# Hybrid attention layer: attention outputs in DRAM per head, with the two contributions as neighbouring rows

## Chip, cores and metric

One Trainium2 chip, one NeuronCore. The metric is the device time of one execution of the whole program in microseconds (us). The time before is the median of three executions, 1822.48 us (1818.33 to 1823.29).

## What is computed

One layer of a decoder trunk over 1024 tokens of width 2048, all in float32. The reference, cut to its outline:

```python
u = rmsnorm(h, norm_pre[l])
proj = jnp.einsum('bsd,de->bse', u, w_in[l])                  # 2048 -> 6656
q_sb, k_sb, v_sb, z_sb, q_sw, k_sw, v_sw, z_sw = jnp.split(proj, SPLIT_POINTS, axis=-1)
o_sb = stick_breaking_attention(q_sb, k_sb, v_sb)             # 16 heads of 64
o_sw = sliding_window_gqa(q_sw, k_sw, v_sw, sinks[l], rel_bias)  # 16 heads, 4 kv heads, window 128
o_sb = rmsnorm(o_sb, gn_sb[l]) * jax.nn.silu(z_sb)
o_sw = rmsnorm(o_sw, gn_sw[l]) * jax.nn.silu(z_sw)
y = jnp.einsum('bse,ed->bsd', jnp.concatenate([o_sb, o_sw], axis=-1), w_out[l])
h = h + rmsnorm(y, norm_post[l])
```

## The kernel before, in words

**Number format.** A matmul of two float32 operands is made of three faster matmuls: each operand is split into a rounded high part and a low rest (`hi`, `lo`; `xh`, `xl`), and hi*hi, hi*lo and lo*hi are added up in PSUM. In attention the high and the low part of a 64-wide head lie side by side on the 128 partitions, so that one matmul takes both.

**Phase 1, projections.** The list `work` (L727) holds 49 blocks of 128 output columns; `proj` (L450) computes each with 96 matmuls of 128x512. Weights come in four pieces of 256 KB per block (`split_w`, L128: a load on SP's queue, a cast on ACT, a subtraction on VectorE). What follows a block depends on its kind: q and k are scaled, split and spilled to DRAM (`split_spill`, L371); v is transposed and kept; z is the gate (`evac_z`, L412).

**Attention in the gaps.** After every three matmuls of a projection `step` (L252) calls `advance` (L148), which places pieces of attention units between the projection matmuls by an estimate of TensorE's time and by written-out lags. A unit has three stages: `s1` makes logits and weights, `s2` transposes the weights on TensorE and splits them, `s3` multiplies them with v into PSUM tile `o`. The order on TensorE is the program's order; on the other engines and on SP's queue, a scheduler orders the instructions at build time, by program order, priorities and its own estimate of when each is ready, and every engine and queue then works strictly in that order. In time, the sliding-window units (`sw`, 64 of them) come first, up to about 490 us, and the stick-breaking units (`sb`, 160) follow, to about 1450 us.

**Attention output, where the change is.** In `s3` the stationary operand is the v tile, of which columns 0 to 63 are the high part of v and 64 to 127 the low part. So the 128 partitions of `o` are two contributions (index r) of 64 rows (e) each, and the head's output is their sum over r. `finish_o` (L488) copies `o` (128x256) on ACT into SBUF tile `ot` (two buffers) and stores it to DRAM tile `od[tile_i]` of shape [2, 128, 1024]: index r, then row head*64+e, then time. It makes one store per contribution, 64 partitions and 64 KB each. A stick-breaking call covers one head and 256 times (`row` given), a sliding-window call two heads and 128 times (`row` is None). There are 64 calls of each kind, so 256 stores.

**Reading it back.** When the z block of the same 128 channels is projected, `load_o` (L406) loads a half (512 times) of `od[tile_i]` as one transfer of 512 KB into SBUF tile `or` (one buffer): 128 partitions, on each of them both contributions. GpSimd (POOL in the profile) then adds the two (L409). `load_o` is called 32 times, twice for each of the 16 z blocks: for half 0 in the middle of the projection (`early`, L707), for half 1 in `evac_z` (L433) after `gate` of half 0 is written. `gate` (L422) multiplies the gate with the sum on VectorE (L424), stores the product to `ogd` (L425, SP's queue), squares the sum on ACT (L429) and adds the squares up on POOL (L430).

**What else stands on the queues.** POOL also sets the first column of each stick-breaking tile `m` (L536), which the scan on VectorE (L542, L545) needs, and adds w_out blocks in a background chain (`sum_job`, L219). SP's queue issues nearly all transfers: weights (L131), q and k of attention (L523, L605, L482), spills (L376, L377), the background chain (L224, L225, L229), `ogd` (L425), `od` (L408, L499).

**Phase 2, output projection.** From about 1510 us on, seven products of quarter matrices (a Strassen-Winograd-like scheme) are computed with `mm_out` (L906); `od` is not used there any more.

Of the kernel before, what the change touches and what calls it, by code (L numbers as in the profile page):

```python
# [23 lines left out]
HALF = 512  # L24
HD = 64
# [32 lines left out]
def layer(ctx, tc, xT, x, w_first, w_blk, w_out, g_pre, g_post, g_sb, g_sw, sinks, rel, onehot, penalty, out):  # L58
    nc = tc.nc
# [4 lines left out]
    od = [dram.tile([2, P, S], F32, name=f"od{i}") for i in range(16)]  # L64
# [340 lines left out]

    def load_o(name, tile_i, h):  # L406
        o2 = stg.tile([P, 2, HALF], F32, tag="or", name=f"or_{name}_{h}", bufs=1)
        nc.sync.dma_start(o2, od[tile_i][:, :, h * HALF:(h + 1) * HALF].rearrange("r p t -> p r t"))  # L408
        nc.gpsimd.tensor_add(o2[:, 0, :], o2[:, 0, :], o2[:, 1, :])  # L409
        return o2[:, 0, :]  # L410

    def evac_z(ps, name, tile_i, gain, grp, last=False):  # L412
        zf, sg = [], []
        for h in range(2):
            zf.append(scaled(ps[h], name, h))
            sg.append(stg.tile([P, HALF], F32, tag="sg", name=f"sg_{name}_{h}"))
            nc.scalar.activation(sg[h], zf[h], AF.Sigmoid)
            nc.vector.scalar_tensor_tensor(zf[h], zf[h], gain, sg[h], op0=ALU.mult, op1=ALU.mult)
        if tile_i % 8 == 0:
            accs[grp] = stg.tile([P, S], F32, tag="acc", name=f"acc_{grp}", bufs=1)  # L420

        def gate(h, o):  # L422
            cols = slice(h * HALF, (h + 1) * HALF)
            nc.vector.tensor_mul(zf[h], zf[h], o)  # L424
            nc.sync.dma_start(ogd[tile_i][:, cols], zf[h])  # L425
            if tile_i % 8 == 0:
                nc.scalar.square(accs[grp][:, cols], o)
            else:
                nc.scalar.square(sg[h], o)  # L429
                nc.gpsimd.tensor_add(accs[grp][:, cols], accs[grp][:, cols], sg[h])  # L430

        gate(0, early_o.pop(name))
        o1 = load_o(name, tile_i, 1)  # L433
        if last:
            gate(1, o1)
        else:
            defer(6.0, lambda: gate(1, o1))
# [50 lines left out]
    def finish_o(ops, name, tile_i, row, cols):  # L488
        ot = at.tile([P, 256], F32, tag="ot", name=f"ot_{name}")
        with tc.high_priority(HURRY):  # L490
            nc.scalar.copy(ot, ops[:, :256])
        for r in range(2):
            src = ot[r * HD:(r + 1) * HD, :]
            if row is None:
                dst = od[tile_i][r, :, cols].rearrange("(h e) t -> e h t", h=2)
                src = src.rearrange("p (h t) -> p h t", h=2)
            else:
                dst = od[tile_i][r, row:row + HD, cols]
            nc.sync.dma_start(dst, src)  # L499

    def units_sb(pair, vst):
        units = []
# [9 lines left out]
    def unit_sb(pair, hh, row, a, c, head, grp, vs):  # L512
# [54 lines left out]
        def s3():  # L567
            if c == a:
                grp["o"] = po(f"o_{nm}")
            for j in range(2):  # L570
                for i, wt in enumerate(me["wt"]):
                    mm(grp["o"][:, :256], vs[:, 2 * c + j, :], wt[:, 2 - 2 * j:4 - 2 * j, :],
                       start=(c == a and j == 0 and i == 0), stop=(c == 3 and j == 1 and i == 1))
            if c == 3:
                finish_o(grp["o"], nm, pair, row, slice(a * 256, (a + 1) * 256))
# [10 lines left out]
    def unit_sw(g, i, hp, head, vg):  # L586
# [59 lines left out]
        def s3():  # L646
            ops = po(f"o_{un}")
            for j in range(nj):
                for r, wt in enumerate(me["wt"]):
                    mm(ops[:, :256], vg[:, i + j, :], wt[:, j, :],  # L650
                       start=(j == 0 and r == 0), stop=(j == nj - 1 and r == 1))
            finish_o(ops, un, 8 + blk, None, slice(i * P, (i + 1) * P))
# [54 lines left out]
    def early(name, tile_i):  # L707
        def f():
            assert not left.get(f"sb{tile_i}", 0)
            early_o[name] = load_o(name, tile_i, 0)  # L710
        return f
# [201 lines left out]
    for i in range(LAST + 1):  # L913
        nxt, src = [], []
        for dc in range(2):
# [15 lines left out]
            for e in range(8):  # L931
# [20 lines left out]
                if i == LAST and dc == 0:  # L952
                    tb, h = divmod(e, 2)
# [58 lines left out]
```

## Time and profile before

| | |
|---|---|
| median of three executions | 1822.48 us |
| the profiled execution | 1825.41 us |
| its span, first to last instruction | 1823.7 us |
| TensorE busy | 1786.3 us, 98% of the span |
| VectorE, ACT, POOL busy | 1242.3, 787.2, 496.2 us |
| mean granted TensorE clock | 0.996 of full speed |
| moved by DMA | 312.50 MB |

The profile is of one execution. A group of instructions is shown as line, engine, operation, output<-inputs, tile shape and count; then busy time, mean duration in ns, and the idle time of the engine just before them with what ended it. `SPq` is SP's queue, `PEld` the weight load of TensorE. "DMA to landing" counts from the start of the issuing instruction until the data has landed. Matmuls are pipelined, so a busy TensorE need not be at its peak, and an engine that is idle without delaying another costs nothing.

### The profile page before, as it was taken

How to read it: one execution, taken by the hardware profiler on the slowest of the kernel's cores; microseconds unless marked ns; L12 is line 12 of the kernel's file. 1: busy time of each engine (PE TensorE's matmuls, PEld its weight loads, DVE VectorE, ACT ScalarE, POOL GpSimd, SP SyncE). 2: the span in 40 equal slices, each digit the busy share in tenths (PEclk: the TensorE clock that was granted, in tenths of full speed). 3: DMA queues.
4: the chain of work that ended last, by engine and by line, in shares of the span. 5: the costliest groups of instructions: out<-in, count | busy, mean ns of one | idle time of the engine just before them, and what ended most of it. 6: DMA issues, size and time to landing. Idle time of an engine off the chain costs nothing. (4 is left out here: it accounts for less than half of the span.)

```text
span 1823.7 us, 27416 instructions
## 1 busy us (share of the span) xinstructions
PE 1786.3 (98%) x9046; PEld 1493.2 (82%) x9046; DVE 1242.3 (68%) x1984; ACT 787.2 (43%) x1696; POOL 496.2 (27%) x648
## 2 busy tenths in 40 slices
PE   8999999999999999999999999999999999999997
PEld 7788778887888888888888888888888877888886
DVE  7558842588557688587676787767868546745876
ACT  7345531355334344343443444434434434445432
POOL 0011121111213234133232332223303214504523
PEclk9999999999999999999999999999999999999999
DMA  7547775576746656466556563454524376533485
GB/s 229 193 143 206 197 202 167 163 205 199 217 145 191 179 159 199 138 191 173 174 163 181 159 183 124 135 176 127 175 76 132 116 227 211 189 107 128 145 248 184
DMA packets 205421, 312.50 MB, mean 171 GB/s; under 512 B 26176, under 2 KB 85728, under 8 KB 205152
## 3 DMA queue, kind: packets, MB, share of 16 engines
q1 hardware_dynamic: 203216, 307.61, 56.1%
q10 hardware_dynamic: 2064, 3.15, 0.5%
q8 instruction: 72, 1.18, 0.3%
q14 instruction: 69, 0.57, 0.1%
HBM read 219.42 MB, written 91.23 MB: 170 GB/s over the span
## 5 line engine op out<-in xcount | busy, mean ns | idle before, releaser
L545 DVE TENSOR_TENSOR_SCAN m_sb<-m_sb,m_sb,zero 128x257 f32<-128x257 f32 x192 | 159.9, 871 | 49.9 <-ACT m_sb L532 46.8
L548 DVE TENSOR_TENSOR b_sb<-b_sb,m_sb 128x512 f32<-128x512 f32 x160 | 128.3, 802 | 25.2 <-POOL b_sb L538 13.8
L532 ACT ACTIVATE m_sb<-z_sb 128x512 f32<-128x512 f32 x160 | 95.9, 600 | 114.4 <-PE z_sb L122 101.6
L542 DVE TENSOR_TENSOR_SCAN m_sb<-m_sb,mask 128x256 f32<-128x256 f32 x128 | 119.0, 967 | 38.6 <-ACT m_sb L532 36.9
L909 PE MATMUL y<-wohi,x 128*128 128x512 f32 x448 | 140.7, 390 | 0.5 <-ACT wohi L774 0.5
L563 ACT CAST wh_sb<-wt_sb 128x512 fp32r<-128x512 f32 (+1 forms) x160 | 87.0, 544 | 116.3 <-PE wt_sb L126 115.9
L909 PE MATMUL y<-wohl,x 128*128 128x512 f32 x576 | 134.4, 393 | 2.4 <-DVE wohl L775 2.4
L564 DVE TENSOR_TENSOR wl_sb<-wt_sb,wh_sb 128x512 fp32r<-128x512 f32 (+1 forms) x160 | 100.5, 631 | 45.4 <-ACT wh_sb L563 44.6
L909 PEld LDWEIGHTS y<-wohl,x 128*128 128x128 f32 x576 | 109.2, 190 | 25.7 <-DVE wohl L775 2.9
L122 PE MATMUL p_zsb<-xh,whi_zsb 128*128 128x512 f32 x256 | 103.9, 406 | 1.6 <-ACT whi_zsb L133 1.4
L122 PE MATMUL p_zsw<-xh,whi_zsw 128*128 128x512 f32 x256 | 104.8, 409 | 0.0
L122 PE MATMUL p_qsb<-xh,whi_qsb 128*128 128x512 f32 x256 | 104.5, 408 | 0.0
L122 PE MATMUL p_ksb<-xh,whi_ksb 128*128 128x512 f32 x256 | 104.4, 408 | 0.0
L122 PE MATMUL p_vsb<-xh,whi_vsb 128*128 128x512 f32 x256 | 102.9, 402 | 0.0
L122 PE MATMUL p_zsb<-xh,wlo_zsb 128*128 128x512 f32 x256 | 101.4, 396 | 1.3 <-DVE wlo_zsb L135 1.3
L122 PE MATMUL p_zsw<-xh,wlo_zsw 128*128 128x512 f32 x256 | 101.4, 396 | 0.0
L122 PE MATMUL p_zsw<-xl,whi_zsw 128*128 128x512 f32 x256 | 101.1, 395 | 0.0
L122 PE MATMUL p_ksb<-xh,wlo_ksb 128*128 128x512 f32 x256 | 101.1, 395 | 0.0
L122 PE MATMUL p_zsb<-xl,whi_zsb 128*128 128x512 f32 x256 | 101.1, 395 | 0.0
L122 PE MATMUL p_qsb<-xh,wlo_qsb 128*128 128x512 f32 x256 | 100.8, 394 | 0.0
L122 PE MATMUL p_ksb<-xl,whi_ksb 128*128 128x512 f32 x256 | 100.8, 394 | 0.0
L122 PE MATMUL p_vsb<-xh,wlo_vsb 128*128 128x512 f32 x256 | 100.6, 393 | 0.0
(242 smaller groups left out, 4926.7 us busy)
## 6 DMA issues: line engine op xcount, KB each, us to landing
row_sw<-in_w_out SPq DMA_DIRECT2D x80, 256.0 KB, 4.3
bg<-in_w_out SPq DMA_DIRECT2D x80, 256.0 KB, 4.2
woraw<-wsum SPq DMA_DIRECT2D x80, 256.0 KB, 3.4
kh<-kd SPq DMA_DIRECT2D x160, 64.0 KB, 3.0
kl<-kd SPq DMA_DIRECT2D x160, 64.0 KB, 2.8
wsum<-row_sw SPq DMA_DIRECT2D x40, 256.0 KB, 2.6
wsum<-bg SPq DMA_DIRECT2D x40, 256.0 KB, 2.8
q_sw<-qd SPq DMA_DIRECT2D x64, 128.0 KB, 3.4
```

What stands on the lines that cost most here:

```text
L122: tc.keep_in_program_order(nc.tensor.matmul(ps, a, b, start=start, stop=stop))
L532: nc.scalar.activation(m[:, :, 1:257], z, AF.Sigmoid, scale=-SCALE)
L542: nc.vector.tensor_tensor_scan(m[:, tb, 1:257], m[:, tb, 1:257], mask[:, P - P * tb:P - P * tb + 256], m[:, tb, 0:1], ALU.mult, ALU.max)
L545: nc.vector.tensor_tensor_scan(m[:, tb, :], m[:, tb, :], zero.to_broadcast([P, 257]), prev[:, tb, 256:257], ALU.mult, ALU.max)
L548: nc.vector.tensor_mul(beta, beta, m[:, :, 0:256])
L563: nc.scalar.copy(wh[:, :k], pt[:, :k])
L564: nc.vector.tensor_sub(wl[:, :k], pt[:, :k], wh[:, :k].bitcast(F32))
L909: nc.tensor.matmul(ps, xt[:, a, tcols], w[b][:, cols], start=first and n == 0, stop=last and n == 2)
```

## The change

`od[tile_i]` keeps its shape [2, 128, 1024], but the first index becomes the head (of the two in a tile) and the row becomes r*64+e: the two contributions of a head are neighbouring rows, as they are on the partitions of `ot`. `finish_o` makes one store of 128 partitions (128 KB) in place of two of 64 partitions. `load_o` makes two loads in place of one: each brings one head, 64 partitions with both contributions on each (256 KB). The addition on POOL and all that follows it stay as they are. In all, 256 stores become 128, and 32 loads become 64; the bytes are the same.

```diff
@@ -405,7 +405,9 @@
 
     def load_o(name, tile_i, h):
         o2 = stg.tile([P, 2, HALF], F32, tag="or", name=f"or_{name}_{h}", bufs=1)
-        nc.sync.dma_start(o2, od[tile_i][:, :, h * HALF:(h + 1) * HALF].rearrange("r p t -> p r t"))
+        for i in range(2):
+            nc.sync.dma_start(o2[i * HD:(i + 1) * HD],
+                              od[tile_i][i, :, h * HALF:(h + 1) * HALF].rearrange("(r e) t -> e r t", r=2))
         nc.gpsimd.tensor_add(o2[:, 0, :], o2[:, 0, :], o2[:, 1, :])
         return o2[:, 0, :]
 
@@ -489,14 +491,10 @@
         ot = at.tile([P, 256], F32, tag="ot", name=f"ot_{name}")
         with tc.high_priority(HURRY):
             nc.scalar.copy(ot, ops[:, :256])
-        for r in range(2):
-            src = ot[r * HD:(r + 1) * HD, :]
-            if row is None:
-                dst = od[tile_i][r, :, cols].rearrange("(h e) t -> e h t", h=2)
-                src = src.rearrange("p (h t) -> p h t", h=2)
-            else:
-                dst = od[tile_i][r, row:row + HD, cols]
-            nc.sync.dma_start(dst, src)
+        if row is None:
+            nc.sync.dma_start(od[tile_i][:, :, cols].rearrange("h p t -> p h t"), ot.rearrange("p (h t) -> p h t", h=2))
+        else:
+            nc.sync.dma_start(od[tile_i][row // HD, :, cols], ot)
 
     def units_sb(pair, vst):
         units = []
```

## Rows read from the trace of the kernel before

**Rows 1.** The page, part 1: busy us, share of the span, instructions.

```profile
PE 1786.3 (98%) x9046; PEld 1493.2 (82%) x9046; DVE 1242.3 (68%) x1984; ACT 787.2 (43%) x1696; POOL 496.2 (27%) x648
```

**Rows 2.** Busy time by stage: us, PE, PEld, DVE, ACT, POOL busy, clock, DMA, GB/s.

```profile
126.00:490.00 364.00, 356.90 (x1877) 296.48 (x1877) 241.43 (x621) 159.61 (x502) 69.77 (x55) 1.00 0.67 191
490.00:1450.00 960.00, 954.58 (x5083) 808.41 (x5082) 686.36 (x931) 414.71 (x788) 285.51 (x488) 1.00 0.53 158
1450.00:1510.00 60.00, 56.27 (x234) 44.22 (x232) 27.36 (x37) 20.54 (x36) 14.25 (x11) 0.97 0.71 228
```

**Rows 3.** What TensorE waited for: us in total, times, longest.

```profile
PE wt_sb L126 <- DVE b_sb L548: 3.0, 2, 2.0
...
PE o_sb L122 <- DVE wl_sb L564: 2.4, 2, 1.2
PE o_sw L122 <- ACT ot_sw L491: 2.2, 5, 1.4
...
PE y L909 <- DVE wolo L775: 1.8, 2, 1.5
PE p_zsb L122 <- ACT whi_zsb L133: 1.4, 1, 1.4
PE p_zsb L122 <- DVE wlo_zsb L135: 1.3, 2, 0.7
PE p_vsw L122 <- ACT whi_vsw L133: 0.9, 1, 0.9
```

**Rows 4.** SP's queue by line, count: issue ns min/median/max; L408's landing.

```profile
L499 SPq DMA_DIRECT2D od<-ot_sw x128: 574/600/1437, 126.4 to 488.7; - x128
L499 SPq DMA_DIRECT2D od<-ot_sb x128: 446/587/1298, 542.4 to 1449.9; - x128
...
L408 SPq DMA_DIRECT2D or_zsw<-od x16: 377/384/737, 143.8 to 1072.3; - x16
L408 SPq DMA_DIRECT2D or_zsb<-od x16: 371/383/433, 1080.2 to 1500.9; - x16
...
DMA to landing us min/median/max: 3.7/4.5/6.0
...
L755 SPq DMA_DIRECT2D woraw<-wsum x80: 319/320/1405, 1479.7 to 1787.2; - x80
```

**Rows 5.** ACT in order of time, end of a sliding-window stretch: start, us [idle before].

```profile
255.38 0.37 ACT L491 COPY ot_sw<-o_sw 128x256 f32<-128x256 f32 x1 [4.42 <-DMA od<-ot_sw]
262.45 0.37 ACT L491 COPY ot_sw<-o_sw 128x256 f32<-128x256 f32 x1 [6.70 <-DMA od<-ot_sw]
```

**Rows 6.** SP, POOL and DVE in order of time around one load of or.

```profile
658.09 0.39 SPq L408 DMA_DIRECT2D or_zsw<-od  x1
...
663.39 1.29 POOL L409 TENSOR_TENSOR or_zsw<-or_zsw 128x512 f32<-128x512 f32 x1 [4.55 <-DMA or_zsw<-od]
664.62 0.10 POOL L536 MEMSET m_sb<- 128x2 f32 x1
...
665.32 2.39 DVE L545 TENSOR_TENSOR_SCAN m_sb<-m_sb,m_sb,zero 128x257 f32<-128x257 f32 x2
```

**Rows 7.** ACT in the last z blocks; idle before in brackets.

```profile
1485.27 0.63 ACT L429 ACTIVATE sg_zsb<-or_zsb 128x512 f32<-128x512 f32 x1 [5.96 <-POOL or_zsb L409]
```

**Rows 8.** Busy time in a stretch after a stall of TensorE; columns as in rows 2.

```profile
669.50:673.20 3.70, 3.70 (x13) 3.12 (x14) 3.60 (x6) 0.59 (x1) 0.58 (x3) 0.54 0.92 282
```

**Rows 9.** DMA issues: count, KB each, median us from issue to landing.

```profile
kh<-kd SPq DMA_DIRECT2D x160, 64.0 KB, 3.0
kl<-kd SPq DMA_DIRECT2D x160, 64.0 KB, 2.8
...
q_sw<-qd SPq DMA_DIRECT2D x64, 128.0 KB, 3.4
...
q_sb<-qd SPq DMA_DIRECT2D x64, 128.0 KB, 3.1
```

## The prediction

> **What bounds the kernel now.** I read the page's busy times first [rows 1]: TensorE works for 98% of the span, VectorE for 68%, ACT for 43%, POOL for 27%. A transfer can only matter where TensorE stands still. The table by stage [rows 2] says how much standing there is where the change acts: 364.00 - 356.90 = 7.1 us in the sliding-window stage, 960.00 - 954.58 = 5.4 us in the stick-breaking stage, 60.00 - 56.27 = 3.7 us in the last z blocks, together 16.2 us, 0.9% of the span. After 1510 us `od` is not used. The list of TensorE's waits [rows 3] then says which stalls an output store or load can reach, and the order of time around them [rows 5 to 7] by what chain. Last come SP's issue times by line [rows 4] and the landing times [rows 9], for the prices.
>
> Two chains reach TensorE.
>
> First, the `ot` chain in the sliding-window stage. ACT may not overwrite one of the two `ot` buffers before its stores have landed. At 255.38 and 262.45 us ACT stood for 4.42 and 6.70 us for that [rows 5], and everything behind it on ACT stood too: TensorE lost 2.2 us waiting for `ot_sw` and 0.9 us for the weight cast `whi_vsw` behind the second wait [rows 3], together 3.1 us.
>
> Second, the `or` chain. POOL's addition of the two contributions waits for the load, and POOL works in order: issued at 658.09, the load let the addition start at 663.39 [rows 6], with the one-column write of `m` behind it at 664.62, and VectorE's scan, which needs that write, began at 665.32. The weights of that unit were late, and TensorE had one of its two waits for `b_sb`, 2.0 us long [rows 3]. In the last z blocks the same load holds ACT: the square of `or` waited 5.96 us for POOL's addition [rows 7], with the cast of the next weights behind it. By this reading six of the 32 loads end in a stall: two in the waits for `b_sb` (3.0 us), two in those for `wl_sb` (2.4), one in the `p_zsb` waits (1.4 + 1.3), one in that for `wolo` (1.8). That is 9.9 us. [...]
>
> **The stores, step by step.** Two issues of 64 partitions go, 600 ns each in the sliding-window stage and 587 in the other [rows 4]. One issue of 128 partitions comes. No row shows exactly it; the nearest are transfers of 128 partitions, 320 ns for `woraw` and 384 ns for `or` [rows 4], and the upper end is the 600 ns of the present stores. I take 384 ns, because `or`, like the new store of two heads, has two runs on each partition. SP's queue gets 128 x (1.19 - 0.38) = 104 us shorter. This is time of a queue, not of TensorE: it counts only where a landing is awaited. In the `ot` chain the pair's second store is issued 0.6 us after the first, and this one lands last; with one store the buffer comes free some 0.6 us earlier, more where several stores stand in a row. Of the 4.42 and 6.70 us most is other work on the queue, so the waits remain, but the stalls on TensorE behind them are short (five of 0.2 to 1.4 us, and one of 0.9). I take 2.0 us of the 3.1 us as gained; ends 0 and 3.1. In the stick-breaking stage no `ot` wait on a store is among TensorE's stalls: nothing gained, nothing lost; two `ot` buffers at 2.5 units per call cover it.
>
> **The loads, step by step.** One issue of 384 ns goes; two of 64 partitions with two runs each come, priced by the present sliding-window stores, which have that form: 600 ns. Per call 0.8 us more on SP, 32 x 0.8 = 26 us in all, so SP gains 104 - 26 = 78 us net. Behind the loads in SP's order stand weight loads, stores and, for half 1, the next `ogd` store, which waits for the gate anyway; 0.8 us later is covered, because TensorE's waits name no weight transfer.
>
> What counts is when the second half has landed, because POOL's addition now waits for both. It is issued 0.6 us after the first. A 64-partition load of 64 KB lands after 2.8 to 3.0 us, one of 128 KB after 3.1 to 3.4 us [rows 9], so 64 KB more cost 0.1 to 0.6 us, in the middle 0.35. For 256 KB that is 3.1 + 2 x 0.1 = 3.3 to 3.4 + 2 x 0.6 = 4.6 us, in the middle 3.25 + 0.7 = 3.95. If the halves don't hinder each other, both are there 0.6 + 3.95 = 4.55 us after the first issue (ends 3.9 and 5.2); the one load takes 4.5 us [rows 4]. So the addition comes 0.05 us later, ends -0.6 and +0.7. If the second half's data must wait for the first's, 4 x 0.35 = 1.4 us less the 0.6 us of lead are added: 0.85 us later. I take 0.3 us, nearer to the first, because the rows hold back-to-back pairs already (both halves of q are issued so) and still show 3.1 to 3.4 us. At six places this is 6 x 0.3 = +1.8 us. The other 26 loads have slack now: no stall shows behind them, and 0.3 us is little against the lags written into the schedule.
>
> **Sum.** -2.0 + 1.8 = -0.2 us. The profiled execution took 1825.4 us, 1.7 us around its span of 1823.7, and 2.9 us more than the median; the difference is carried to the median: 1822.3 us. With each term at its ends: 1822.5 - 3.1 - 6 x 0.6 = 1815.8 and 1822.5 - 0 + 6 x 0.85 = 1827.6. A measurement of this kernel tells about 0.3%, 5.5 us, from no change.
>
> **Rivals.** *No change that can be measured* is the forecast. For it: the change reaches only 13 us of stalls, and touches them with opposite signs. 0.61, with what follows under another order and under a missed saving.
>
> *The halves go one after the other, and the `or` chain decides: slower.* Place: POOL's addition L409, with the `m` write and the scan behind it in the stick-breaking stage, ACT's square in the last z blocks. With the highest rate of the rows, 0.6 us for 64 KB, the second half lands at 0.6 + 4.6 + (2.4 - 0.6) = 7.0 us, 2.5 later than now; with the middle one 0.85. Halfway, 1.7 us, gives 6 x 1.7 - 2.0 = +8.2: 1830.7 us. It decides from 1.25 us on (6 x 1.25 - 2.0 = 5.5). For it: 64 partitions pay 0.35 us for 64 KB more; against it: the q pairs. 0.13. [...]
>
> *The shorter SP queue pulls more than that: faster.* All 3.1 us of the `ot` chain go, the loads land 0.6 us earlier because less stands around them (-3.6), and the stall before 669.5 us shrinks until the clock holds (-1.7): 1822.5 - 8.4 = 1814.1 us. For it: SP gives back 78 us, and the DMA engines are busy for 0.67 of the sliding-window stage [rows 2]. Against it: both `or` halves are issued later than one. 0.18.
>
> *Another order.* The scheduler places SP's, ACT's, VectorE's and POOL's instructions by its estimate, and 96 fewer issues may deal them anew. That can move each of the 16.2 us of stalls in either direction, mostly by less than 5.5 us: 0.04 to faster, 0.04 to slower, the rest in "same".
>
> *It doesn't do what it says:* the merged store still costs 600 ns to issue. SP then saves 128 x 0.59 - 26 = 49 us instead of 78 and the `ot` gain halves: 1823.3 us, within no change.
>
> **How the numbers follow.** Faster 0.18 + 0.04 = 0.22, slower 0.13 + 0.04 = 0.17, same 0.61. The forecast is the likeliest case's 1822.3. The range takes in the ends of its terms, 1815.8 and 1827.6, and reaches up and down into the rivals, 1815 to 1829, which leaves out the greater part of either.
>
> **What would show it.** Right: 128 stores `od<-ot` at L499's place with 0.32 to 0.43 us each, 64 loads at about 0.6; additions on POOL that start within half a microsecond of where they do now, counted from the first issue (4 to 5.5 us); waits of ACT for `od<-ot_sw` below 21 us but not gone; TensorE's idle time between 126 and 1510 us still 10 to 20 us, its busy time unchanged. Wrong: a POOL addition 1.25 us or more later after its load, with more waits of TensorE for `b_sb` and `wl_sb`; or the sliding-window stage's 7.1 us of idle time nearly gone together with the stall at 667 us; or new waits for weights.

## The result, and the profile after

The changed kernel takes 1806.09 us, the median of six executions (1802.40 to 1812.01). The kernel before, measured beside it, takes 1822.88 us (six, 1818.33 to 1827.01). The ratio is 0.9916, 95% interval 0.9891 to 0.9941: 0.9% faster. The forecast was 1822.3 us, 1815 to 1829, so the result lies 9 us below the range.

The profiled execution took 1807.31 us, its span 1805.6 us. First the page's busy times and the table by stage, in the windows and columns of [rows 1, 2]:

```profile
PE 1780.6 (99%) x9046; PEld 1492.2 (83%) x9046; DVE 1245.8 (69%) x1984; ACT 789.6 (44%) x1696; POOL 496.0 (27%) x648
```

```profile
126.00:490.00 364.00, 360.74 (x1910) 302.32 (x1909) 248.15 (x626) 162.61 (x509) 73.28 (x58) 1.00 0.69 198
490.00:1450.00 960.00, 958.39 (x5106) 811.89 (x5105) 687.31 (x935) 418.70 (x791) 284.33 (x488) 1.00 0.55 158
1450.00:1510.00 60.00, 59.58 (x256) 47.49 (x255) 27.93 (x39) 24.50 (x43) 10.39 (x8) 1.00 0.86 266
```

TensorE's idle time in the three windows is 3.3, 1.6 and 0.4 us, together 5.3 us, where it was 16.2 us [rows 2]. The windows are fixed in time and the changed kernel runs ahead of the old one, so they don't hold quite the same work. To compare equal work I cut the run at four of TensorE's instructions. The rows are the tile views of both kernels on TensorE. The two times behind the duration are the starts of the first and the last matmul; the kernel before comes first:

```profile
L122 PE MATMUL z_sw<-kh,q_sw x128: 277/282/357, 110.3 to 466.9; 128*128 128x256 f32 x128
L122 PE MATMUL z_sb<-kh,q_sb x320: 278/282/285, 517.1 to 1433.9; 128*128 128x256 f32 x160
L122 PE MATMUL o_sb<-wh_sb,v_vsb x320: 278/282/415, 530.1 to 1448.5; 128*128 128x256 f32 x160
L122 PE MATMUL rms_sb<-acc_sb,mask x4: 592/620/667, 1524.4 to 1525.8; 128*128 128x512 f32 x4
```

```profile
L122 PE MATMUL z_sw<-kh,q_sw x128: 278/279/355, 112.0 to 462.5; 128*128 128x256 f32 x128
L122 PE MATMUL z_sb<-kh,q_sb x320: 278/282/285, 512.4 to 1423.8; 128*128 128x256 f32 x160
L122 PE MATMUL o_sb<-wh_sb,v_vsb x320: 278/282/285, 525.5 to 1438.4; 128*128 128x256 f32 x160
L122 PE MATMUL rms_sb<-acc_sb,mask x4: 592/621/667, 1506.7 to 1508.1; 128*128 128x512 f32 x4
```

**Stage A** is from the first `z_sw` to the first `z_sb` (sliding window): 517.1 - 110.3 = 406.8 us before, 400.4 after. **Stage B** runs from there to the last `o_sb` (stick-breaking): 931.4 and 926.0. **Stage C** runs from there to the first `rms_sb` (last z blocks): 75.9 and 68.3. So A gave 6.4, B 5.4 and C 7.6 us. Ahead of A 1.7 us were lost, behind C 0.4 won, and that makes the 18.1 us between the spans. The gain is in all three stages.

What TensorE still waited for inside the stages, in the columns of [rows 3]:

```profile
PE wt_sw L126 <- DVE L_sw L629: 2.4, 4, 1.1
...
PE o_sb L122 <- DVE wl_sb L562: 1.6, 3, 0.9
PE o_sw L122 <- ACT ot_sw L493: 0.7, 1, 0.7
...
PE y L907 <- DVE wolo L773: 0.3, 1, 0.3
```

Gone are the waits for `b_sb`, for `p_zsb` and for `whi_vsw`; that for `ot_sw` fell from 2.2 to 0.7 us. SP's issues (columns as in [rows 4]) and the landing times of the loads (as in [rows 9]):

```profile
L495 SPq DMA_DIRECT2D od<-ot_sw x64: 365/382/1216, 128.1 to 482.7; - x64
L497 SPq DMA_DIRECT2D od<-ot_sb x64: 319/382/1601, 538.0 to 1439.3; - x64
L409 SPq DMA_DIRECT2D or_zsw<-od x32: 585/603/1125, 142.9 to 1064.0; - x32
L409 SPq DMA_DIRECT2D or_zsb<-od x32: 585/600/621, 1073.3 to 1485.7; - x32
```

```profile
or_zsw<-od SPq DMA_DIRECT2D x32, 256.0 KB, 4.6
...
or_zsb<-od SPq DMA_DIRECT2D x32, 256.0 KB, 4.3
```

The merged store costs SP 0.38 us and each load 0.60 us, as taken. But each half load takes as long as the whole one did, 4.3 to 4.6 us, and it is often issued late. SP in order of time:

```profile
1073.30 0.60 SPq L409 DMA_DIRECT2D or_zsb<-od  x1
...
1080.82 0.60 SPq L409 DMA_DIRECT2D or_zsb<-od  x1
```

These are the two halves of one pair, 7.5 us apart. Of the 32 pairs nine stand apart on SP's queue, six of them by 5 to 9 us. Counted over all 32, both halves have landed 5.84 us (median) after the first issue, where the one load took 4.47, and POOL's addition starts 6.0 us after it, where it was 4.6. **The loads got worse, and the kernel got faster.** The place of [rows 6] shows how. POOL in order of time, then VectorE, then ACT:

```profile
656.60 0.10 POOL L534 MEMSET m_sb<- 128x2 f32 x1 [2.60 <-DVE m_sb L543]
658.72 1.43 POOL L411 TENSOR_TENSOR or_zsw<-or_zsw 128x512 f32<-128x512 f32 x1 [2.01 <-DMA or_zsw<-od]
```

```profile
657.66 1.39 DVE L543 TENSOR_TENSOR_SCAN m_sb<-m_sb,m_sb,zero 128x257 f32<-128x257 f32 x2
659.16 1.53 DVE L546 TENSOR_TENSOR b_sb<-b_sb,m_sb 128x512 f32<-128x512 f32 x1
660.61 0.68 DVE L426 TENSOR_TENSOR u_zsw<-u_zsw,or_zsw 128x512 f32<-128x512 f32 x1
```

```profile
657.61 0.62 ACT L133 CAST whi_zsw<-wraw_zsw 128x512 fp32r<-128x512 f32 x1 [0.70 <-PE p_zsw L122]
660.18 0.64 ACT L431 ACTIVATE sg_zsw<-or_zsw 128x512 f32<-128x512 f32 x1 [1.95 <-POOL or_zsw L411]
```

The addition still starts 5.46 us after its first load (issued at 653.26), before it was 663.39 - 658.09 = 5.30 us. But the write of `m`, which stood behind the addition [rows 6], now stands ahead of it. On VectorE the scan and the `b_sb` multiplication stand ahead of the gate's multiplication, which must wait for the addition, and on ACT the weight cast stands ahead of the square, which waits too. Before, all were the other way round; VectorE and ACT of the kernel before, in order of time:

```profile
664.71 0.69 DVE L424 TENSOR_TENSOR u_zsw<-u_zsw,or_zsw 128x512 f32<-128x512 f32 x1 [2.13 <-POOL m_sb L536]
665.32 2.39 DVE L545 TENSOR_TENSOR_SCAN m_sb<-m_sb,m_sb,zero 128x257 f32<-128x257 f32 x2
```

```profile
664.71 0.63 ACT L429 ACTIVATE sg_zsw<-or_zsw 128x512 f32<-128x512 f32 x1 [2.97 <-POOL m_sb L536]
665.25 0.60 ACT L133 CAST whi_zsw<-wraw_zsw 128x512 fp32r<-128x512 f32 x1
```

The same engines wait as before, but at this place nothing that TensorE needs is queued behind them. The stall of 2.0 us is gone, and with it the stretch at a granted clock of 0.54 [rows 8]: the changed kernel has 1.00 from 652 to 670 us. The same holds in the last z blocks: the square that had waited 5.96 us [rows 7] waits 1.91 us, none there waits over 2.62 us, and TensorE's stalls in stage C shrink to 0.3 us.

Who changed the order? The text of the program orders TensorE alone; POOL, VectorE, ACT and SP are ordered by the scheduler at build time. Compared instruction by instruction, the built programs have the same order on TensorE, but 24 instructions of POOL, 47 of VectorE and 36 of ACT stand elsewhere. So my theory was: **the new transfers are a loss or nothing in B and C, and the new order, a by-product, is the gain.** The rival: the transfers themselves (the shorter SP queue) are the gain, and the order is idle.

### The profile page after: what moved, and what is told of

It is laid out like the page before. It is cut to its first block, busy times and chain, and to the rows that moved or that the text cites. A ratio compares the mean times of both kernels' runs of the same rounds, so it can differ in the third digit from the quotient of the medians.

```text
span 1805.6 us, 27329 instructions
## 1 busy us (share of the span) xinstructions
PE 1780.6 (99%) x9046; PEld 1492.2 (83%) x9046; DVE 1245.8 (69%) x1984; ACT 789.6 (44%) x1696; POOL 496.0 (27%) x648
## 5 line engine op out<-in xcount | busy, mean ns | idle before, releaser
L623 ACT ACTIVATE L_sw<-L_sw,nm_sw 128x256 f32<-128x256 f32 (+1 forms) x128 | 62.6, 490 | 91.6 <-DVE nm_sw L618 88.5
L122 PE MATMUL p_qsb<-xl,whi_qsb 128*128 128x512 f32 x256 | 100.6, 393 | 0.0
```

What stands on the lines that cost most here:

```text
L122: tc.keep_in_program_order(nc.tensor.matmul(ps, a, b, start=start, stop=stop))
L623: nc.scalar.activation(L[:, hh, :n], L[:, hh, :n], AF.Exp, bias=nm[:, hh:hh + 1], accum_out=sm[:, hh:hh + 1])
```

## Experiments

In most of them the order on POOL, VectorE and ACT is written out as a list of places per engine, and an edge that only orders (`NoSync` in the diff) ties each instruction to its neighbour in the list, so that transfers and order can be exchanged separately. SP's queue is left to the scheduler, except in e12 and e13:

```diff
+def pin_order(nc, tc):
+    for engine, order in ORDER.items():
+        mine = [i for i in nc.cur_bb.bb.instructions
+                if str(i.engine).rsplit(".", 1)[-1] == engine and str(i.opcode) in OPCODES]
+        mine = [None] * (len(order) - len(mine)) + mine
+        seq = [mine[k] for k in order if mine[k] is not None]
+        for a, b in zip(seq, seq[1:]):
+            tc.add_manual_dep(b, a.name, mybir.DependencyInfo(mybir.DependencyClass.NoSync, mybir.DependencyReason.DATA),
+                              reason="pin_order")
```

All results, with A, B and C read from the same four rows as above (of one profiled execution each; ratios are to the kernel before, run beside it, whose medians were 1819.4 to 1820.7 us, and are not quotients of two medians: e9's two, 1808.67 and 1819.81, are 0.6% apart):

| run | transfers | order on POOL, VectorE, ACT | median us | ratio, 95% interval | A | B | C |
|---|---|---|---|---|---|---|---|
| before | old | old | 1822.88 | | 406.8 | 931.4 | 75.9 |
| after | new | new | 1806.09 | 0.9916, 0.9891 to 0.9941 | 400.4 | 926.0 | 68.3 |
| e1 | old | new | 1812.31 | 0.9947, 0.9926 to 0.9969 | 410.3 | 924.4 | 68.4 |
| e2 | new | old | 1872.86 | 1.0290, 1.0249 to 1.0331 | 400.4 | 986.1 | 74.7 |
| e3 | loads by 64 partitions | free (a third one) | 1814.67 | 0.9969, 0.9952 to 0.9985 | 404.2 | 930.0 | 71.4 |
| e4 | loads by contribution | free (the old one) | 1820.93 | 0.9998, 0.9981 to 1.0015 | 406.1 | 932.5 | 75.5 |
| e5 | merged stores, loads by contribution | free | 2096.58 | 1.1523, 1.1492 to 1.1554 | 406.8 | 1161.2 | 121.0 |
| e6 | as e5 | new | 2019.16 | 1.1096, 1.1071 to 1.1122 | 405.5 | 1092.4 | 113.1 |
| e7 | new | free (the new one) | 1803.96 | 0.9917, 0.9892 to 0.9942 | 397.6 | 926.3 | 68.7 |
| e8 | old | POOL new | 1820.91 | 1.0001, 0.9987 to 1.0016 | 404.8 | 928.1 | 74.9 |
| e9 | old | old in A, new from B on | 1808.67 | 0.9925, 0.9904 to 0.9946 | 404.7 | 924.0 | 67.4 |
| e10 | old | as e9 without ACT | 1812.26 | 0.9953, 0.9932 to 0.9974 | 407.1 | 925.1 | 72.8 |
| e11 | new loads, old stores | new | 1821.69 | 1.0005, 0.9990 to 1.0020 | 412.9 | 931.7 | 69.6 |
| e12 | new, pairs adjacent | new | 1805.03 | 0.9921, 0.9904 to 0.9937 | 397.6 | 926.2 | 71.9 |
| e13 | new, pairs adjacent | old | 1824.90 | 1.0030, 1.0009 to 1.0050 | 398.0 | 940.6 | 77.5 |

How far A, B and C wander without a cause can be seen in *after* and e7, which turned out to be the same program twice (below): 2.8 us in A, 0.4 us in B and C, 2 us in the median. That is one pair only, and the profiled execution of the kernel before, 1825.41 us, is 2.5 us above its median.

### Transfers and order exchanged: e1 and e2

e1 is the kernel before with `pin_order` and the changed kernel's lists. e2 is the changed kernel with the lists of the kernel before.

> The stores and loads of the kernel before, unchanged; POOL, VectorE and ACT pinned to the order in which the changed kernel has them. Theory order (the gain is the new order of these three engines, not the transfers): about 1806 us like the changed kernel, 1800 to 1811, since one load lands sooner than two; TensorE's idle time between 126 and 1510 us below 8 us instead of 16. Theory queue (the gain is SP's queue being shorter by 128 issues and the earlier landings that follow): about 1823 us, 1818 to 1828, with the idle time of before.

> The stores and loads of the changed kernel; POOL, VectorE and ACT pinned to the order of the kernel before. Theory order: the stalls of before come back, and as POOL's addition starts about 1.2 us later after its load, six of them are longer: 1820 to 1832 us, likeliest 1825. Theory queue: about 1806 us, 1801 to 1811.

e1 keeps the old transfers, and B and C are as short as in the changed kernel, even shorter in B (924.4 and 926.0). Stage A is longer than in the kernel before. e2 has the new transfers in the old order: A has the whole gain (400.4), C hardly any, and B is 55 us longer than before. TensorE's waits in stage B of e2, and one of them in order of time on SP, POOL, VectorE and TensorE:

```profile
PE o_sb L264 <- DVE wl_sb L704: 41.9, 9, 7.6
PE wt_sb L268 <- DVE b_sb L688: 4.2, 4, 2.3
```

```profile
1102.27 0.60 SPq L551 DMA_DIRECT2D or_zsb<-od  x1
...
1110.39 0.60 SPq L551 DMA_DIRECT2D or_zsb<-od  x1
```

```profile
1115.36 1.26 POOL L553 TENSOR_TENSOR or_zsb<-or_zsb 128x512 f32<-128x512 f32 x1 [12.20 <-DMA or_zsb<-od]
...
1116.61 0.62 POOL L678 TENSOR_SCALAR_AFFINE_SELECT b_sb<-b_sb 128x512 f32<-128x512 f32 x1
```

```profile
1117.26 0.69 DVE L688 TENSOR_TENSOR b_sb<-b_sb,m_sb 128x512 f32<-128x512 f32 x1 [9.78 <-POOL b_sb L678]
```

```profile
1118.61 0.58 PE L264 MATMUL o_sb<-wl_sb,v_vsb 128*128 128x256 f32 x1 [7.63 <-DVE wl_sb L704]
```

Read it from the bottom: TensorE waits for `wl_sb`, VectorE stood in order behind a multiplication that waits for POOL's select, POOL stood in order behind the addition, and the addition waits for a half load that was issued 8.1 us after its partner. Half loads are harmful where the old order stands; in the new one, with the merged stores, B is 1.6 us longer than with whole loads (926.0 and 924.4). The theory holds for B and C, with a condition that e11 shows below; the rival holds for A.

### What made the scheduler change its mind: e3 and e4

Both keep the old layout and the old stores and split the load in two: e3 by 64 partitions, as the change does, e4 by contribution, 128 partitions each.

```diff
-        nc.sync.dma_start(o2, od[tile_i][:, :, h * HALF:(h + 1) * HALF].rearrange("r p t -> p r t"))
+        for i in range(2):
+            rows = slice(i * HD, (i + 1) * HD)
+            nc.sync.dma_start(o2[rows], od[tile_i][:, rows, h * HALF:(h + 1) * HALF].rearrange("r p t -> p r t"))
```

```diff
-        nc.sync.dma_start(o2, od[tile_i][:, :, h * HALF:(h + 1) * HALF].rearrange("r p t -> p r t"))
+        for r in range(2):
+            nc.sync.dma_start(o2[:, r, :], od[tile_i][r, :, h * HALF:(h + 1) * HALF])
```

> Old layout and old stores; only the load is split into two of 64 partitions with two runs each. The order of POOL is then that of the changed kernel, that of VectorE and ACT partly. Theory order: the stick-breaking stage and the last z blocks gain what they gain in the changed kernel (5.5 and 7.7 us), the sliding-window stage (6.1 us there) little: 1807 to 1813 us, likeliest 1810. Theory queue: SP has 25 us more to issue and the loads land later: 1823 to 1830 us.

> Old layout and old stores; the load is split into two of 128 partitions, one per contribution. The order on POOL, VectorE and ACT is exactly that of the kernel before. Theory order: no change, 1819 to 1827 us. A theory that two smaller loads by themselves help (the first data move while the second is issued): below 1815 us, POOL's addition more than 0.5 us earlier after the first issue.

e4's built order on POOL, VectorE and ACT is the old one without exception, and so is its time. e3's order on POOL is exactly the changed kernel's; on VectorE 26 and on ACT 14 instructions still differ from it. It gets part of the gain, 0.3%. So two loads alone change nothing, and two of 64 partitions make the scheduler put the addition later on POOL. That it reckons with a later landing for them is my reading and not shown. The merged stores move the rest.

### Which engine's order: e8, e10, e9

All three are the kernel before with lists: e8 with the new list for POOL alone; e9 with lists for all three that follow the old order up to the first stick-breaking unit and the new one from there; e10 with the lists of e9 for POOL and VectorE, ACT left to the scheduler.

> The kernel before with POOL alone pinned to the changed kernel's order; VectorE keeps the order of before, ACT nearly. Theory POOL (the write of m behind the addition is what stalls): the stick-breaking stage gains most of its 5 to 7 us, the last z blocks nothing, as ACT holds those: 1815 to 1818 us. Rival (VectorE's multiplication in gate, which waits for the same addition ahead of the scan, holds it as well): under 2 us gained, 1820 to 1825.

> The stores and loads of the kernel before. POOL, VectorE and ACT keep the order of the kernel before up to the first stick-breaking unit and are pinned to the changed kernel's order from there on. Theory (after the sliding-window stage the gain is order alone): the stick-breaking stage and the last z blocks gain 5 to 8 us each, 1808 us, 1805 to 1812. Rival (the new transfers have a part there): above 1814.

> As the run before it, but ACT is left to the scheduler, which gives it nearly the order of the kernel before. Theory (POOL and VectorE decide in the stick-breaking stage, ACT in the last z blocks): the stick-breaking stage gains 5 to 8 us as there, the last z blocks under 3 us: 1814 us, 1811 to 1818. Rival (POOL and VectorE suffice for both): 1808.

POOL alone gives nothing in the median and 3.3 us in B: with the addition out of the way of `m`, VectorE still has the gate's multiplication ahead of the scan, and the stalls for `b_sb` stay. POOL and VectorE together give B (925.1). ACT's order gives most of C (72.8 with two engines, 67.4 with three). TensorE's waits between 520 and 1510 us in e9:

```profile
PE o_sb L264 <- DVE wl_sb L706: 0.3, 1, 0.3
PE y L1051 <- DVE wolo L917: 0.2, 1, 0.2
```

That is the whole list: with the old transfers and the new order, half a microsecond of the 9.9 us of [rows 3] is left in these stages. The new order by itself is worth 0.75% by the ratio (interval 0.54 to 0.96%), 11 us between the medians (1808.67 and 1819.81 us).

### The stores: e11, e5 and e6

e11 is the changed kernel in the new order, with two stores per call again (in the new layout). e5 was to isolate the merged stores in another way: new layout and merged stores, but loads by contribution, which e4 had shown to leave the order alone. e6 is e5 in the new order.

```diff
-            nc.sync.dma_start(od[tile_i][row // HD, :, cols], ot)
+        for r in range(2):
+            rows = slice(r * HD, (r + 1) * HD)
...
+                nc.sync.dma_start(od[tile_i][row // HD, rows, cols], ot[rows, :])
```

```diff
-        for i in range(2):
-            nc.sync.dma_start(o2[i * HD:(i + 1) * HD],
-                              od[tile_i][i, :, h * HALF:(h + 1) * HALF].rearrange("(r e) t -> e r t", r=2))
+        for r in range(2):
+            nc.sync.dma_start(o2[:, r, :], od[tile_i][:, r * HD:(r + 1) * HD, h * HALF:(h + 1) * HALF])
```

> The changed kernel, its layout and its two loads, with two stores of 64 partitions in place of the merged one; POOL, VectorE and ACT pinned to the changed kernel's order. Theory (the merged stores give the sliding-window stage's gain): that stage 6 to 10 us longer than in the changed kernel, the others as there, 1814 us, 1810 to 1818. Rival (the stage gains by order): 1806 within 3 us.

> The changed kernel's layout and merged stores; each load_o call makes two loads of 128 partitions, one per contribution. The order on the three engines is then nearly that of the kernel before. Theory (the stores give the sliding-window stage's gain of about 6 us, the order the rest): 1816 us, 1812 to 1820; the sliding-window stage 5 to 7 us shorter, the stick-breaking stage and the last z blocks within 2 us of before. Rival (the order gives it in all stages): 1822, no stage over 2 us shorter. Rival (the layout itself helps): 1806.

> As the run before it, with POOL, VectorE and ACT pinned to the order of the changed kernel. Theory: both gains, and loads that land over 1 us earlier than the changed kernel's: 1800 to 1807 us, likeliest 1804, the changed kernel's time or a little less. Rival (the later landing is harmless in that order): 1806 within 3 us.

e11 loses everything: 1821.69 us, with A at 412.9 and B at 931.7. Leaving out e5 and e6, A with the old stores in the old order is 404.7 to 407.1 (before, e4, e8, e9, e10; mean 405.9; e3, in a third order, has 404.2), with the merged stores in either order 397.6 to 400.4 (after, e2, e7, e12, e13; mean 398.8). That is 7.1 us for the merged stores, whatever the order. e5 and e6 have the merged stores too, and A is 406.8 and 405.5 there. Their one pair of loads in this stage is slow (below): in e5 POOL's addition starts 16.4 us after the first issue. Behind it TensorE stalls for 2.4 us (e6: 2.3) for `ot_sw` near 158 us and for 2.7 us (2.9) for a transfer of q or k near 181 us; no other run has such stalls. That the slow loads cause them is my reading.

With old stores in the new order A is 410.3 and 412.9 (e1, e11). By my estimate part of that is TensorE's clock: from 110 to 510 us the granted clock is 0.99 in e1 and 0.98 in e11, where the kernel before and e12 have 1.00. The longest stall for `ot_sw` is 2.5 us in e1 and 2.0 us in e11 (before: 1.4). So the new order doesn't pay there without the merged stores; how much is order and how much is clock isn't separated. The waits in stage A of e11 and of e12, a run with merged stores in the same order:

```profile
PE wt_sw L268 <- DVE L_sw L774: 7.7, 7, 1.5
PE o_sw L264 <- ACT ot_sw L635: 3.9, 3, 2.0
```

```profile
PE wt_sw L319 <- DVE L_sw L822: 1.3, 3, 0.5
```

The waits for `ot_sw` go with the merged stores, and most of those for `L_sw`, a tile that VectorE writes. The second isn't settled: e2, with merged stores in the old order, still has 3.6 us of `L_sw` waits and an A of 400.4.

The stores matter in B as well. In the same new order B is 924.4 us with whole loads and old stores (e1), 926.0 to 926.3 with half loads and merged stores (after, e7, e12), and 931.7 with half loads and old stores (e11): there the half loads cost 7.3 us and the order's gain is gone. TensorE's main wait in stage B of e11, and POOL ahead of the longest stall (3.3 us, until 734.6):

```profile
PE o_sb L264 <- DVE wl_sb L707: 4.8, 2, 3.3
```

```profile
730.29 1.29 POOL L369 TENSOR_TENSOR bg<-bg 128x512 f32<-128x512 f32 x1 [6.15 <-DMA bg<-in_w_out]
731.53 0.62 POOL L681 TENSOR_SCALAR_AFFINE_SELECT b_sb<-b_sb 128x512 f32<-128x512 f32 x1
```

The select that the unit's weights need stands behind an addition of the background chain, whose load is late. In e11 that load is issued at 724.72: earlier transfers of the chain go first, and POOL's addition for these stands behind an `or` addition that waited 6.4 us, until 717.41. In e1 the load is issued at 715.05, and POOL waits 0.53 us for it. So the new order, too, has a place where TensorE's work stands behind a wait. The changed kernel stalls there for 0.9 us; why the merged stores keep it short isn't shown.

e5 and e6 fell far from what was expected, and for a reason of their own. In the new layout a load by contribution has the two heads as its outer dimension in DRAM. One of POOL's additions of e5, in order of time:

```profile
648.62 1.26 POOL L410 TENSOR_TENSOR or_zsw<-or_zsw 128x512 f32<-128x512 f32 x1 [12.44 <-DMA or_zsw<-od]
```

The pair was issued at 635.33, so the addition came 13.3 us after it, against 4.6 us before (medians over all 32: 14.3 and 4.6). 512 KB in 13.3 us is some 40 GB/s. A stretch in which SP has issued nothing behind the pair, columns as in [rows 2]:

```profile
637.20:638.80 1.60, 0.52 (x3) 0.55 (x4) 1.50 (x4) 0.72 (x2) 0.00 (x0) 0.50 0.13 42
```

The DMA share of 0.13 is the time of 2.1 of the core's 16 engines, at 42 GB/s. So these two runs don't isolate the stores; they show that the form of the load in DRAM decides: e4's pairs, by contribution too but from the old layout, have landed 4.3 us after the first issue, where e5's addition starts 14.3 us after it (medians). Why so few engines are busy is not shown.

### Whether the late second loads cost: e7, e12, e13

What was still open is whether e2's 55 us came from the pairs as such or from the second loads that the scheduler had put up to 8 us behind the first. e7 was meant to bring them together in the changed kernel, by asking for program order:

```diff
-            nc.sync.dma_start(o2[i * HD:(i + 1) * HD],
+            ld = nc.sync.dma_start(o2[i * HD:(i + 1) * HD],
                               od[tile_i][i, :, h * HALF:(h + 1) * HALF].rearrange("(r e) t -> e r t", r=2))
+            if i:
+                BG(ld)
```

> The changed kernel, with the second load of each call held directly behind the first on SP's queue (in the changed kernel it stands up to 8 us later in seven calls). The order on the other engines is the changed kernel's. Theory (what counts is where the waiting instructions stand, and those seven have slack): 1803 to 1809 us, no change against the changed kernel. Rival (the late second loads cost TensorE time): 1798 to 1803.

The request had no effect: the built order is the changed kernel's on every engine and on SP's queue. So e7 is a repetition, and what was expected of it was not tried. e12 and e13 write SP's queue out too, with every second load directly behind the first, and are otherwise the changed kernel and e2.

```diff
+    "SP": _runs("""
...
+"""),
```

> The changed kernel, its order on POOL, VectorE and ACT written out, and on SP's queue the second load of each pair directly behind the first (nine pairs stand apart in the changed kernel). Theory (in the new order nothing that TensorE needs stands behind the addition): a load that is complete up to 7 us earlier is worth nothing, 1802 to 1809 us, stick-breaking stage 925 to 927 us. Rival (late second loads still cost in the new order, and hide part of the gain): below 1800 us, stick-breaking stage under 923 us.

> As the run with the new transfers in the old order, but on SP's queue the second load of each pair directly behind the first (ten pairs stood up to 8 us apart there). Theory (the 55 us of that run were the second loads that came late, in an order where the weights stand behind the addition): most of it goes; pairs complete some 1.3 us later than the one load did cost at the six places of the prediction some 8 us, less 6.4 us in the sliding-window stage: 1817 to 1832 us, stick-breaking stage 931 to 945 us. Rival (the pair itself is what costs in the old order): stays above 1850 us, stick-breaking stage above 965 us.

With the pairs adjacent, both halves have landed 5.2 us (median) after the first issue. In the new order that is worth nothing: e12 is at 1805.03 us, *after* and its repetition at 1806.09 and 1803.96. (Its C of 71.9 holds a stall of 2.4 us for a weight of phase 2, `wohi`, and a granted clock of 0.98; *after* has neither, and no run says why.) In the old order it is worth 45 us: B falls from 986.1 to 940.6 us. What is left is the price of the pair as such, 940.6 - 931.4 = 9.2 us in B and 1.6 us in C. TensorE's waits in stage B of e13, and its busy time from 520 to 1430 us (columns as in [rows 2]):

```profile
PE o_sb L315 <- DVE wl_sb L755: 5.8, 4, 2.6
PE wt_sb L319 <- DVE b_sb L739: 4.1, 4, 2.0
```

```profile
520.00:1430.00 910.00, 899.91 (x4794) 761.23 (x4793) 652.27 (x891) 393.87 (x750) 267.18 (x471) 0.99 0.53 156
```

Eight stalls of 9.9 us stand where four of 5.4 us stood [rows 3], and the granted clock is 0.99 where the kernel before has 1.00 in this window. Here it is shown that the new loads cost where something stands behind the addition.

## Why the prediction was wrong

**The step that failed** is the one that took the order as given. The sum moved six stalls by the shift of the load and left everything else in its place; *Another order* was let in with 0.04 to faster and the words that it moves the stalls "mostly by less than 5.5 us". e9 shows it at 7.4 us in B and 8.5 us in C, some 16 us in one execution each and 11 us between the medians, without a single transfer changed. It was the largest effect of this change, and it isn't a shift of stalls but their removal: [rows 6, 7] showed which instructions stood behind the waiting ones, and an order that puts those first ended nearly all of the six stalls (9.9 us, of which e9 has 0.5); the granted clock, 0.54 behind one of them [rows 8], is 1.00 at this place in e9 (653 to 665 us). The prediction had this sum on the page and didn't ask what a scheduler would do with it.

**How far the rest was right** can be read from e13, which is the kernel that the prediction had in mind: old order, both loads back to back. It takes 1824.90 us, within the range and 2.6 us from the forecast. But that is luck: against the kernel before beside it (1819.36 us; ratio 1.0030, 1.0009 to 1.0050) it is slower, where the sum had -0.2 us, and two errors of opposite sign stand in it:
- The `ot` term was taken as -2.0 us, ends 0 and -3.1. Measured in A: -7.1 us on the mean, -6.4 in the changed kernel. The sign and the chain were right: TensorE's waits for `ot_sw` fell from 2.2 to 0.7 us. ACT's own waits for `od<-ot_sw` fell from 21.8 to 18.0, which tells little, as e4, with the old stores and order, has 13.4. The waits for `whi_vsw` (0.9) went, and those for `L_sw` fell from 3.7 to 2.4. Together with these the idle time of the window shrinks by 3.8 us; the rest of A's gain lies in TensorE's busy time, and no run here says why.
- The `or` term was taken as 0.3 us at six places, +1.8 us, with 0.85 as the upper end. Measured with adjacent pairs: the addition starts 5.34 us after the first issue where it was 4.60, so 0.74 us, near that upper end. The six places were wrong, too: with 0.74 us of lateness new ones appear, and B and C lose 10.8 us. "The other 26 loads have slack" was the weak sentence. It also took the pairs as adjacent; nine are not.

**The prices on SP** were right: 0.38 and 0.60 us. The rival of a shorter SP queue was right in A, and by more than it claimed. Its other two claims were wrong: the loads land later and not earlier, and the stall before 669.5 us [rows 8] went because of the order, not because of the queue: e9, with the old queue, has no wait for `b_sb`, and e13, with the shorter queue in the old order, still has one of 2.0 us. The -1.7 us in its sum is my estimate from [rows 8], 3.7 us at a granted clock of 0.54, so 3.7 x 0.46; no run shows that a shorter stall keeps the clock up, and behind one of 1.9 us it was 1.00 in one execution and 0.57 in another (last section). The slower rival, one half after the other, is what e13 shows in B, though at 0.74 us of lateness and not at the 1.25 us and more that it was to need; the new order hides it in the changed kernel.

**Put together:** stores 7.1 us in A, the new order some 16 us in B and C, the new loads in the new order some 2 us back (B 926.0 to 926.3 against 924.0 and 924.4). The sum, about 21 us, is more than the 16.8 us between the medians and the 18.1 us between the spans; 1.7 us went ahead of stage A (below), and the stage times are of single executions. The parts also don't simply add up: with the old stores put back (e11) the whole gain goes, and with the old order put back (e2, e13) it goes as well. The gain needs both.

## What to carry to other kernels

Where a scheduler orders the queues at build time, an edit to a transfer is also an edit to its inputs: before pricing the transfer, compare the built order of every engine, and for each instruction that waits for a transfer list what stands behind it on its engine. In these runs what a wait cost was set by what was queued behind it: the same half loads cost 55 us, 9 us, 7 us or 2 us. If the order is what counts, write it out: the old transfers with three reordered queues gave 0.75%, most of the gain.

## What was unexpected in the hardware

A load of 64 partitions took as long to land here as one of twice the bytes on 128: 4.3 to 4.6 us for 256 KB, against 4.5 us for 512 KB [rows 4]. A pair of loads of 128 partitions and 256 KB each (e4) had landed 4.3 us after the first issue, a pair of 64 partitions (e13) 5.2 us.

The same stall was followed by a lower clock in one execution and not in another. At 88 us TensorE waits 1.9 us for a v tile in both kernels. Busy time from 90 to 94 us, before and after, columns as in [rows 2]:

```profile
90.00:94.00 4.00, 3.91 (x20) 3.32 (x21) 1.45 (x3) 1.26 (x3) 1.86 (x2) 1.00 0.69 202
```

```profile
90.00:94.00 4.00, 3.79 (x12) 3.19 (x13) 1.52 (x4) 1.26 (x3) 1.96 (x2) 0.57 0.76 198
```

The granted clock was 1.00 before; after, it was 0.57, and 0.50 from 91 to 93 us, with 12 matmuls in place of 20. Nothing in the change touches this place, and e12, with the same order, kept 1.00 there. By the clock that costs 4 x 0.43 = 1.7 us, which is what the profiled execution lost ahead of stage A (112.0 against 110.3 us), and a reason not to count on a single profile for effects of that size.
